# RMSNorm mean squares by a float32r product with a matrix of ones, and the last norm's scalings placed between the last products, in a two-layer hybrid decoder step

## The chip, the cores and the metric

The kernel runs on one core of a Trainium2 chip. The metric is the time of one execution on the device, in microseconds (us). A difference of 0.2% is about what can be told from none.

## What is computed

One inference step of a decoder with two layers, for a new sequence of 1024 tokens and eight samples of eight tokens, 1088 tokens in all, at a model width of 1024 in float32. Each layer is a token mixer (layer 0 an RG-LRU block with a convolution of width four, layer 1 chunked gated linear attention, GLA), a cross-attention over 256 memory tokens, and an MLP with a squared ReLU. In front of each of these six parts stands an RMSNorm, and one more at the end:

```python
def rmsnorm(x, g):
    y = x * lax.rsqrt(jnp.mean(x * x, axis=-1, keepdims=True) + EPS)
    return y * g

for layer in range(2):
    x = x + mixer[layer](rmsnorm(x, norm_mix_g[layer]))
    x = x + cross_attn(rmsnorm(x, norm_xa_g[layer]), mem_k[layer], mem_v[layer])
    x = x + square(relu(rmsnorm(x, norm_mlp_g[layer]) @ w1[layer])) @ w2[layer]
y = rmsnorm(x, final_norm_g)
```

A seventh norm of the same kind, of the memory, is made once at the start and isn't touched by the change.

## The kernel before

The residual `x` lies transposed in SBUF: 128 partitions by eight row tiles m (8 x 128 = 1024 features) by tokens, in three column blocks c of 384, 384 and 320 tokens (`x[c]`; the last holds 256 tokens of the sequence and the 64 of the samples). Products are made in three passes of float32r (`mm3`, L99 to L101): the high part of the weights (`whi`) by the high part of the data (`xh` or `hh`), by its low part (`xl`, `hl`), and the low part of the weights (`wlo`) by the high. Weights stream in as units of 512 KB, are split by ScalarE (L186, high) and VectorE (L187, low), and four split units are held at a time. A mixer's or MLP's out-product (`gemm_out`) is queued and run later, while the next in-product goes on; it adds each row tile into `x[c]` (L279) from one of three PSUM banks `pb`, so a bank is free for the next tile only when that add is done.

The norm is folded into the products: `norm_tile` (L297 on) squares a tile (ScalarE, L302 and L305), adds it to an accumulator `acc[c]` over the eight tiles (L306: GpSimd, and VectorE for tiles 3 and 7), and writes the tile times the gain g as `xh` (L311) and `xl` (L312). The inverse root is multiplied in behind the next product. It is made in two steps that `norm_end` puts into a queue of deferred calls (`after`, `tick`):

- `rstd_sum` (L332 to L341), two ticks later: for each 128 tokens a product of `acc` with the column `ones` (1/1024) sums over the partitions (L336) and leaves the mean squares by token, one per partition. `inv_rms` takes the inverse root of these few columns with Ln and Exp (ScalarE, L324 and L325) and one Newton step (VectorE, L327 to L330) into `rtok`.
- `rstd_row` (L343 to L351), one tick later: transposes of `rtok`, spread over 128 columns, give the same number on all partitions (L347), which ScalarE copies to `rstd[c]` (L348).

The last norm, V_FIN, has no product behind it. There `norm_tile` multiplies the gain into `x` itself (ScalarE, L309), and `finish` (L353 to L359) multiplies by `rstd[c]` tile by tile (L357: GpSimd for tiles 0 and 4, VectorE for the others) and stores four tiles at a time (L359: two stores of 768 KB for a wide block, of 640 KB for the last) from SyncE's queue. `mlp(1, V_FIN)` queues these last out-products; they run at the end one block after the other.

The order of instructions on an engine isn't the order of the Python calls: a scheduler places them by its own estimate of when their inputs are ready, unless a dependency forces an order.

## Time and profile before

| | |
|---|---|
| time, three runs | median 3048.1 us, 3046.98 to 3052.01 |
| the profiled execution | 3050.53 us |
| its span, first to last instruction | 3048.8 us |
| mean granted clock of TensorE | 0.994 of full speed |
| TensorE busy / weight loads busy | 98% / 96% of the span |
| VectorE / ScalarE / GpSimd busy | 57% / 34% / 6% |
| HBM traffic | 63 GB/s over the span |

The profile is that of one execution; its rows give starts in us from the span's first instruction, and durations. TensorE's matrix part is PE, its weight loads PEld, VectorE DVE, ScalarE ACT, GpSimd POOL, SyncE SP. Matrix instructions overlap in the pipeline, so a product's cost is read from the distance of two starts, not from its own duration. The granted clock is told as a share of full speed: 1.00 is 2.4 GHz, 0.50 is 1.2 GHz. A bracket behind a row gives the idle time of the engine before it and what ended it. L numbers are lines of the kernel before; the tables of instructions in the next section that are marked as the new order's have the lines of the changed file.

### The profile page before, as it was taken

Reading aid. Unit: us, or ns where it says so; the run is one execution under the profiler, and the core shown is the slowest. Engines: PE = TensorE matmul, PEld = TensorE weight load, DVE = VectorE, ACT = ScalarE, POOL = GpSimd, SP = SyncE. Lnnn points to the kernel's source line nnn. Section 1 sums busy time; section 2 is a strip of 40 time slices with the busy share of each in tenths; the row PEclk is TensorE's granted clock in tenths of the full one; section 3 lists DMA queues with packets and bytes.
Section 4 is the critical chain, followed back from the end, with each engine's and each line's share of the span. In section 5 each row is a group of like instructions: output and inputs, shape, how many; then the busy total and the mean of one; then the engine's idle time right before and its main releaser. Section 6 shows DMA issues by size and latency. Waiting matters only on the chain.

```text
span 3048.8 us, 45853 instructions
## 1 busy us (share of the span) xinstructions
PE 2999.3 (98%) x18923; PEld 2920.6 (96%) x18923; DVE 1752.6 (57%) x3304; ACT 1038.8 (34%) x1907; POOL 193.6 (6%) x267
## 2 busy tenths in 40 slices
PE   8999999999999999999999999999999999999997
PEld 8999999999999999999999999899999999999997
DVE  7577786566444444444664564765574444444445
ACT  7555573234121111112543343642251211112114
POOL 4100020001000000000200000100020000000002
PEclk9999999999999999999999999999999999999998
DMA  8311113332111111111211212143221111111111
GB/s 276 121 44 44 42 61 98 98 100 63 42 42 56 42 42 42 44 54 35 57 54 32 70 32 70 44 124 95 87 77 42 49 49 42 42 42 50 48 42 59
DMA packets 155778, 194.82 MB, mean 64 GB/s; under 512 B 11280, under 2 KB 140560, under 8 KB 155568
## 3 DMA queue, kind: packets, MB, share of 16 engines
q1 hardware_dynamic: 152768, 182.82, 19.5%
q0 software_dynamic: 2800, 9.06, 0.8%
q8 instruction: 148, 2.42, 0.3%
q14 instruction: 62, 0.51, 0.1%
HBM read 178.34 MB, written 13.52 MB: 63 GB/s over the span
## 4 chain that ended last, share of the span: by engine, by line
PE 91%; DVE 4%; ACT 2%; DMA 1%; issue 1%; POOL 0%; DVEq 0%; SPq 0%; ACTq 0%; POOLq 0%
PE pa L101 13%; PE pa L99 13%; PE pa L100 13%; PE pb L99 9%; PE pb L101 9%; PE pb L100 9%; PE pm L99 5%; PE pm L100 5%; PE pm L101 5%; PE pa L262 1%; DMA kvt<-in_cache_v 1%; PE pa L263 1%; PE pa L264 1%; DVE xl L312 1%; PE pb L800 1%
## 5 line engine op out<-in xcount | busy, mean ns | idle before, releaser
L99 PE MATMUL pa<-xh,whi 128*128 128x384 f32 (+2 forms) x2528 | 827.1, 327 | 0.7 <-ACT xh L311 0.7
L100 PE MATMUL pa<-xl,whi 128*128 128x384 f32 (+2 forms) x2528 | 825.1, 326 | 2.7 <-DVE xl L312 2.7
L101 PE MATMUL pa<-xh,wlo 128*128 128x384 f32 (+2 forms) x2528 | 827.4, 327 | 0.0
L279 DVE TENSOR_TENSOR x<-x,pb 128x384 f32<-128x384 f32 (+1 forms) x792 | 412.4, 528 | 209.4 <-PE pb L101 208.5
L99 PE MATMUL pb<-hh,whi 128*128 128x384 f32 (+1 forms) x1584 | 525.2, 332 | 3.2 <-DVE x L279 2.2
L101 PE MATMUL pb<-hh,wlo 128*128 128x384 f32 (+1 forms) x1584 | 519.6, 328 | 0.0
L100 PE MATMUL pb<-hl,whi 128*128 128x384 f32 (+1 forms) x1584 | 519.3, 328 | 0.0
L186 ACT CAST whi<-raw 128x1024 fp32r<-128x1024 f32 (+1 forms) x250 | 256.8, 1040 | 680.8 <-PE pa L100 357.7
L100 PEld LDWEIGHTS pa<-xl,whi 128*128 128x128 f32 x2528 | 475.7, 188 | 4.6 <-DVE xl L312 3.9
L99 PEld LDWEIGHTS pa<-xh,whi 128*128 128x128 f32 x2528 | 475.8, 188 | 2.6 <-ACT xh L311 1.0
L101 PEld LDWEIGHTS pa<-xh,wlo 128*128 128x128 f32 x2528 | 475.6, 188 | 1.0 <-DVE wlo L187 0.7
L187 DVE TENSOR_TENSOR wlo<-raw,whi 128x1024 fp32r<-128x1024 f32 (+1 forms) x250 | 304.6, 1229 | 242.2 <-ACT whi L186 239.3
L679 DVE SCALAR_TENSOR_TENSOR r<-pa,rstd 128x384 f32<-128x384 f32 (+1 forms) x192 | 102.3, 534 | 399.4 <-PE pa L101 398.7
L99 PEld LDWEIGHTS pb<-hh,whi 128*128 128x128 f32 x1584 | 299.0, 189 | 13.2 <-DVE x L279 6.6
L680 ACT ACTIVATE r<-r 128x768 f32<-128x768 f32 (+1 forms) x96 | 77.6, 808 | 674.4 <-DVE r L679 674.4
L100 PEld LDWEIGHTS pb<-hl,whi 128*128 128x128 f32 x1584 | 298.9, 189 | 0.3 <-DVE hl L546 0.3
L101 PEld LDWEIGHTS pb<-hh,wlo 128*128 128x128 f32 x1584 | 298.7, 189 | 0.1
L279 DVE TENSOR_TENSOR x<-x,pm 128x320 f32<-128x320 f32 (+1 forms) x360 | 190.9, 530 | 111.7 <-PE pm L101 111.6
L306 POOL TENSOR_TENSOR acc<-acc,sq 128x384 f32<-128x384 f32 (+1 forms) x105 | 118.1, 1125 | 2055.0 <-ACT sq L305 2040.8
L99 PE MATMUL pm<-hh,whi 128*128 128x320 f32 (+1 forms) x720 | 234.8, 326 | 0.0
L101 PE MATMUL pm<-hh,wlo 128*128 128x320 f32 (+1 forms) x720 | 234.8, 326 | 0.0
L100 PE MATMUL pm<-hl,whi 128*128 128x320 f32 (+1 forms) x720 | 234.7, 326 | 0.0
(310 smaller groups left out, 3940.0 us busy)
## 6 DMA issues: line engine op xcount, KB each, us to landing
raw<-in_mlp_w SPq DMA_DIRECT2D x128, 512.0 KB, 3.8
kvt<-in_cache_kT SPq DMA_DIRECT2D x64, 256.0 KB, 4.9
kvt<-in_cache_v SPq DMA_DIRECT2D x64, 256.0 KB, 5.0
raw<-in_xa_wv SPq DMA_DIRECT2D x16, 512.0 KB, 5.0
raw<-in_rg_w_in SPq DMA_DIRECT2D x16, 512.0 KB, 3.6
raw<-in_xa_wq SPq DMA_DIRECT2D x16, 512.0 KB, 3.5
raw<-in_xa_wo SPq DMA_DIRECT2D x16, 512.0 KB, 3.6
raw<-in_gla_w_in SPq DMA_DIRECT2D x16, 512.0 KB, 3.7
```

The lines of the kernel that those rows point to most:

```text
L99: mm(out, lh, rh, start=first, stop=False)
L100: mm(out, lh, rl, start=False, stop=False)
L101: mm(out, ll, rh, start=False, stop=last)
L186: nc.scalar.copy(hi[:, o], raw[:, o])
L187: nc.vector.tensor_sub(lo[:, o], raw[:, o], f32(hi[:, o]))
L262: mm(out, self.xh[c][:, k, xs], hv[:, kk, :], start=k == 0, stop=False)
L263: mm(out, self.xh[c][:, k, xs], lv[:, kk, :], start=False, stop=False)
L264: mm(out, self.xl[c][:, k, xs], hv[:, kk, :], start=False, stop=k == 7)
L279: nc.vector.tensor_add(x, x, p[:, :per * w].rearrange("p (m t) -> p m t", m=per))
L306: (nc.vector if m % 4 == 3 else nc.gpsimd).tensor_add(self.acc[c][:, :w], self.acc[c][:, :w], sq[:, :w])
L679: nc.vector.scalar_tensor_tensor(r[:, f], p[f][:, :w], 0.0, self.rstd[c], op0=OP.max, op1=OP.mult)
L680: nc.scalar.activation(r, r, AF.Square)
```

## The change

For the six inner norms the sum over the partitions is made by a square matrix of ones (`ones_r`, 128 x 128, value 1/1024) in float32r: `acc` is split into a high part `ah` (ScalarE) and a low part `al` (VectorE), two products of the block's width put the mean squares by token on all 128 partitions at once, and Ln, Exp and a Newton step in three operations of the block's width make `rstd[c]` directly. There is no `rtok` and there are no transposes; GLA's norm (V_MIX + 1), whose values are scaled by token, takes `rtok` back from `rstd` with one column of the identity (`rstd_col`). A forced order without a semaphore (`in_order`) keeps the first of the two products behind the last `mm3` issued before it.

The last norm is rearranged. Blocks 0 and 1 keep the old sum and transposes (`tok_sum`, `tok_row`), but these and the scalings (`piece`) are called from a table between the row tiles of the next block's out-product: block 0's between those of block 1 and the first of block 2, block 1's sum and transposes between those of block 2. The last block takes a full-precision product with the square of ones, and its scalings follow, behind block 1's. The gain is multiplied in together with `rstd` by one VectorE operation (L418 of the new file); only the tiles scaled by GpSimd (`on_pool`: 0 and 4 of block 0; 0, 2, 4 and 6 of block 1) still have it multiplied in by ScalarE. Block 1's accumulations are all GpSimd's. Stores are of two tiles: twelve of 393 or 328 KB (768 and 640 KB halved) where there were six.

```diff
         mm(out, lh, rl, start=False, stop=False)
-        mm(out, ll, rh, start=False, stop=last)
+        self.last_mm = mm(out, ll, rh, start=False, stop=last)
...
                     self.norm_tile(c, m, norm)
+                    if norm == V_FIN and c:
+                        self.between[c, m]()
         if last:
...
             nc.scalar.activation(sq[:, :w], x, AF.Square)
-            (nc.vector if m % 4 == 3 else nc.gpsimd).tensor_add(self.acc[c][:, :w], self.acc[c][:, :w], sq[:, :w])
+            self.last_acc = (nc.vector if m % 4 == 3 and (c, norm) != (1, V_FIN) else nc.gpsimd).tensor_add(self.acc[c][:, :w], self.acc[c][:, :w], sq[:, :w])
         g = self.vec[:, m, norm:norm + 1]
         if norm == V_FIN:
-            nc.scalar.activation(x, x, AF.Copy, scale=g)
+            if self.on_pool(c, m):
+                nc.scalar.activation(x, x, AF.Copy, scale=g)
         else:
...
         self.normed[c] = norm
-        self.after(2, lambda: self.rstd_sum(c, norm))
+        if norm != V_FIN:
+            self.after(2, lambda: self.rstd_sum(c, norm))
+        elif c == 0:
+            self.after(2, lambda: self.tok_sum(0))
+            self.last_pieces()
+        elif c == NC - 1:
+            self.rstd_sum(c, norm)
...
+        nc, w = self.nc, WID[c]
+        acc, r = self.acc[c][:, :w], self.rstd[c]
+        p = self.pm()[:, :w]
+        if norm == V_FIN:
+            nc.tensor.matmul(p, f32(self.ones_r), acc, start=True, stop=True)
+            for m in range(NK):
+                self.piece(1, m)
+        else:
+            ah, al = (self.sp.tile([128, MAXW], R32, name=n, tag="sq", bufs=2)[:, :w] for n in ("ah", "al"))
+            nc.scalar.copy(ah, acc)
+            nc.vector.tensor_sub(al, acc, f32(ah))
+            self.in_order(nc.tensor.matmul(p, self.ones_r, ah, start=True, stop=False))
+            nc.tensor.matmul(p, self.ones_r, al, start=False, stop=True)
+        nc.scalar.activation(r, p, AF.Ln, bias=self.eps)
+        nc.scalar.activation(r, r, AF.Exp, scale=-0.5)
+        u = self.sp.tile([128, MAXW], F32, name="nu", tag="acc", bufs=2)[:, :w]
+        nc.vector.scalar_tensor_tensor(u, p, EPS, r, op0=OP.add, op1=OP.mult)
+        nc.vector.scalar_tensor_tensor(u, u, -0.5, r, op0=OP.mult, op1=OP.mult)
+        nc.vector.scalar_tensor_tensor(r, u, 1.5, r, op0=OP.add, op1=OP.mult)
+        if norm == V_MIX + 1:
+            self.after(1, lambda: self.rstd_col(c, norm))
+            return
+        self.rstd_done[c] = norm
+        if norm == V_FIN:
+            self.finish(c)
+    def rstd_col(self, c, norm):
...
         for i, (j, t0, tw) in enumerate(TILES[c]):
-            nc.tensor.matmul(p[:tw, i:i + 1], self.acc[c][:, t0:t0 + tw], self.ones, start=True, stop=True)
+            nc.tensor.matmul(p[:tw, i:i + 1], self.rstd[c][:, t0:t0 + tw], self.ident[:, 0:1], start=True, stop=True)
+        j0, n = TILES[c][0][0], len(PTILES[c])
+        nc.vector.tensor_copy(self.rtok[:, j0:j0 + n], p[:, 0:n])
+        if c == NC - 1:
+            nc.vector.tensor_copy(self.rtok[:64, 8:9], p[:64, n:n + 1])
+        self.rstd_done[c] = norm
+    def in_order(self, mm):
+        if self.last_mm is not None:
+            self.tc.add_manual_dep(mm.ins, self.last_mm.ins.name, mybir.DependencyInfo(
+                mybir.DependencyClass.NoSync, mybir.DependencyReason.DATA), reason="order")
+    def tok_sum(self, c):
+        nc = self.nc
+        p = self.pm()
+        for i, (j, t0, tw) in enumerate(TILES[c]):
+            mm = nc.tensor.matmul(p[:tw, i:i + 1], self.acc[c][:, t0:t0 + tw], self.ones, start=True, stop=True)
+            if i == 0:
+                self.in_order(mm)
         j0, n = TILES[c][0][0], len(PTILES[c])
         self.inv_rms(self.rtok[:, j0:j0 + n], p[:, 0:n], 128, n)
-        if c == NC - 1:
-            self.inv_rms(self.rtok[:, 8:9], p[:64, n:n + 1], 64, 1)
-        self.after(1, lambda: self.rstd_row(c, norm))
-    def rstd_row(self, c, norm):
+    def tok_row(self, c):
         nc, w = self.nc, WID[c]
         p = self.pm()
-        for j, t0, tw in TILES[c]:
-            nc.tensor.transpose(p[:, t0:t0 + tw], self.rtok[:tw, j:j + 1].to_broadcast([tw, 128]), self.ident[:tw, :tw])
+        for i, (j, t0, tw) in enumerate(TILES[c]):
+            mm = nc.tensor.transpose(p[:, t0:t0 + tw], self.rtok[:tw, j:j + 1].to_broadcast([tw, 128]), self.ident[:tw, :tw])
+            if i == 0:
+                self.in_order(mm)
         nc.scalar.copy(self.rstd[c], p[:, :w])
-        self.rstd_done[c] = norm
-        if norm == V_FIN:
-            self.finish(c)
+    def on_pool(self, c, m):
+        return c < 2 and m % (4, 2)[c] == 0
+    def piece(self, c, m):
+        nc, w = self.nc, WID[c]
+        x = self.x[c][:, m, :]
+        if self.on_pool(c, m):
+            nc.gpsimd.tensor_mul(x, x, self.rstd[c])
+        else:
+            mul = nc.vector.scalar_tensor_tensor(x, x, self.vec[:, m, V_FIN:V_FIN + 1], self.rstd[c], op0=OP.mult, op1=OP.mult)
+            if c == 1:
+                self.tc.add_manual_dep(mul.ins, self.last_acc.ins.name, mybir.DependencyInfo(
+                    mybir.DependencyClass.NoSync, mybir.DependencyReason.DATA), reason="order")
+        if m % 2:
+            nc.sync.dma_start(self.a.yT[:, m - 1:m + 1, COL[c]:COL[c] + w], self.x[c][:, m - 1:m + 1, :])
+    def last_pieces(self):
+        do = lambda m: lambda: self.piece(0, m)
+        no = lambda: None
+        first = [no, lambda: self.tok_row(0), no, do(0), do(1), do(2), do(4), do(3)]
+        then = [do(5), no, do(6), no, lambda: self.tok_sum(1), do(7), lambda: self.tok_row(1), no]
+        self.between = {(c, m): fn for c, fns in ((1, first), (2, then)) for m, fn in enumerate(fns)}
     def finish(self, c):
-        nc, w = self.nc, WID[c]
         for m in range(NK):
-            x = self.x[c][:, m, :]
-            (nc.vector if m % 4 else nc.gpsimd).tensor_mul(x, x, self.rstd[c])
-            if m % 4 == 3:
-                nc.sync.dma_start(self.a.yT[:, m - 3:m + 1, COL[c]:COL[c] + w], self.x[c][:, m - 3:m + 1, :])
+            self.piece(c, m)
...
         make_identity(nc, self.ident)
-        self.ones = cp.tile([128, 1], F32, name="ones")
-        nc.vector.memset(self.ones, 1.0 / D)
+        self.ones_r = cp.tile([128, 128], R32, name="ones_r")
+        nc.vector.memset(f32(self.ones_r), 1.0 / D)
+        self.ones = f32(self.ones_r)[:, 0:1]
+        self.last_mm = None
         self.eps = cp.tile([128, 1], F32, name="eps")
```

How the change moves instructions is shown at three places, as the built programs have them, one row for each instruction or for equal ones in a row, first before and then now.

TensorE at the first norm end, that of block 0 of the first norm, among the products of the memory's keys (`mh`, `ml` are the memory's halves, `whi`, `wlo` the weights', `acc` the summed squares). Before:

```order
L459 MATMUL pa<-wlo,mh 128x256
L460 MATMUL pa<-whi,ml 128x256
L336 MATMUL pm<-ones,acc 128x1 x3
L458 MATMUL pb<-whi,mh 128x256
L459 MATMUL pb<-wlo,mh 128x256
```

and now, with the lines of the new file (L537 to L539 are the old L458 to L460):

```order
L538 MATMUL pa<-wlo,mh 128x256
L539 MATMUL pa<-whi,ml 128x256
L354 MATMUL pm<-ah,ones_r 128x384
L355 MATMUL pm<-al,ones_r 128x384
L537 MATMUL pb<-whi,mh 128x256
L538 MATMUL pb<-wlo,mh 128x256
```

The three products of one column are now two of 384 columns, at the same place; the transposes some fifty products later have no row any more.

ScalarE where the first gates of the RG-LRU layer are computed (L600, new L679: sigmoids into `rt`, `it`) and the last block's root of the first norm (`irms`, `rtok`; now `rstd`) falls between. Before:

```order
L324 ACTIVATE irms<-pm,eps 128x2
L325 ACTIVATE rtok<-irms 128x2
L600 ACT_TABLE_LOAD
L600 ACTIVATE rt<-pm,vec 128x384
L324 ACT_TABLE_LOAD
L324 ACTIVATE irms<-pm,eps 64x1
L600 ACT_TABLE_LOAD
L600 ACTIVATE it<-pm,vec 128x384
L325 ACT_TABLE_LOAD
L325 ACTIVATE rtok<-irms 64x1
L586 CAST xch<-xc 128x768
L600 ACT_TABLE_LOAD
```

and now:

```order
L665 CAST xch<-xc 128x768
L356 ACTIVATE rstd_97<-pm,eps 128x320
L357 ACTIVATE rstd_97<-rstd_97 128x320
L679 ACT_TABLE_LOAD
L679 ACTIVATE rt<-pm,vec 128x384
L679 ACTIVATE it<-pm,vec 128x384
L679 ACTIVATE rt<-pm,vec 128x384
L679 ACTIVATE it<-pm,vec 128x384
L684 ACT_TABLE_LOAD
```

Logarithm and exponential of the root now stand ahead of the first load, and the four sigmoids behind it in a row; over the whole program there are 50 loads where there were 54.

VectorE in the last products (`x_86`, `x_87`, `x_88` are blocks 0, 1 and 2 of the residual, `pb` the products' banks). Before, block 0's scalings (L357) stood together behind block 1's adds (L279):

```order
L279 TENSOR_TENSOR x_87<-x_87,pb 128x384 x3
L357 TENSOR_TENSOR x_86<-x_86,rstd_95 128x384 x3
L306 TENSOR_TENSOR acc<-acc,sq 128x384
L357 TENSOR_TENSOR x_86<-x_86,rstd_95 128x384 x3
L279 TENSOR_TENSOR x_88<-x_88,pb 128x320 x3
L327 SCALAR_TENSOR_TENSOR irms_28554<-pm,rtok 128x3
L279 TENSOR_TENSOR x_88<-x_88,pb 128x320
L328 TENSOR_TENSOR irms_28554<-irms_28554,rtok 128x3
```

and now they go between the adds (L418), behind the split of `r` into `hl`; the last two rows, one scaling and one add, come six times over in all:

```order
L339 TENSOR_TENSOR rtok<-rtok,irms_28227 128x3
L279 TENSOR_TENSOR x_87<-x_87,pb 128x384
L761 TENSOR_TENSOR hl<-r,hh 128x2x320
L279 TENSOR_TENSOR x_87<-x_87,pb 128x384
L418 SCALAR_TENSOR_TENSOR x_86<-x_86,vec,rstd_95 128x384
L279 TENSOR_TENSOR x_87<-x_87,pb 128x384
```

At the very end VectorE now runs:

```order
L339 TENSOR_TENSOR rtok<-rtok,irms_28399 128x3
L279 TENSOR_TENSOR x_88<-x_88,pb 128x320 x2
L308 TENSOR_TENSOR acc<-acc,sq 128x320
L418 SCALAR_TENSOR_TENSOR x_87<-x_87,vec,rstd_96 128x384 x4
L360 SCALAR_TENSOR_TENSOR nu<-pm,rstd_97 128x320
L361 SCALAR_TENSOR_TENSOR nu<-nu,rstd_97 128x320
L362 SCALAR_TENSOR_TENSOR rstd_97<-nu,rstd_97 128x320
L418 SCALAR_TENSOR_TENSOR x_88<-x_88,vec,rstd_97 128x320 x8
```

The scalings of block 0 are through before block 2's adds begin, and all eight of block 2 are VectorE's.

## Rows read from the trace of the kernel before

**Rows 1.** The page, engines: busy us, share, instructions.

```profile
PE 2999.3 (98%) x18923; PEld 2920.6 (96%) x18923; DVE 1752.6 (57%) x3304; ACT 1038.8 (34%) x1907; POOL 193.6 (6%) x267
```

**Rows 2.** Timeline, TensorE near 450 us: start, us, operation, out<-in, shape, count.

```profile
449.97 0.33 PE L101 MATMUL pa<-xh,wlo 128*128 128x384 f32 x1
450.14 0.72 PE L336 MATMUL pm<-ones,acc 128*128 128x1 f32 x6
450.73 0.40 PE L99 MATMUL pb<-hh,whi 128*128 128x320 f32 x1
```

**Rows 3.** Timeline, TensorE near 453 and 739 us.

```profile
453.04 0.51 PE L347 MATMUL pm<-ident,rtok 128*128 128x128 f32 x3
453.39 0.71 PE L774 MATMUL pm<-ident,P 128*128 128x128 f32 x5
...
739.07 0.58 PE L347 MATMUL pm<-ident,rtok 128*128 128x128 f32 x3
739.58 0.41 PE L99 MATMUL pa<-xh,whi 128*128 128x320 f32 x1
```

**Rows 4.** Timeline, TensorE near 52 us; brackets: idle time, releaser.

```profile
52.23 0.87 PE L347 MATMUL pm<-ident,rtok 128*128 128x128 f32 x3 [3.79 <-DVE rtok L330]
52.75 0.56 PE L458 MATMUL pa<-whi,mh 128*128 128x256 f32 x1
```

**Rows 5.** Windows: us, busy (count) PE, PEld, DVE, ACT, POOL, PEclk, DMA, GB/s.

```profile
48.00:52.00 4.00, 0.44 (x4) 0.24 (x3) 4.00 (x8) 4.00 (x10) 2.89 (x3) 0.98 1.02 334
52.00:55.20 3.20, 2.97 (x14) 3.00 (x15) 3.20 (x7) 2.72 (x6) 1.36 (x2) 0.50 0.71 232
...
154.00:161.00 7.00, 6.11 (x19) 5.79 (x20) 7.00 (x21) 5.62 (x9) 1.31 (x4) 0.52 0.48 150
```

**Rows 6.** Timeline, TensorE near 153 us.

```profile
153.09 0.45 PE L99 MATMUL pm<-xch,gwh 128*128 128x384 f32 x1 [3.00 <-ACT rt L600]
...
154.89 0.69 PE L99 MATMUL pb<-hh,whi 128*128 128x384 f32 x1 [1.00 <-ACT hh L545]
```

**Rows 7.** Timeline, TensorE at the last sum.

```profile
3031.45 1.14 PE L336 MATMUL pm<-ones,acc 128*128 128x1 f32 x6 [1.79 <-DVE acc L306]
```

**Rows 8.** Weight load of L336 near 713 us; L336's idle time (us, times).

```profile
713.04 0.30 PEld L336 LDWEIGHTS pm<-ones,acc 128*128 128x128 f32 x2 [0.50 <-DVE acc L306]
...
  DVE acc L306: 10.6, 8
```

**Rows 9.** Timeline, ScalarE, 130 to 138 us: first and last table load.

```profile
132.30 1.28 ACT L324 ACT_TABLE_LOAD   x1
...
138.01 1.28 ACT L600 ACT_TABLE_LOAD   x1
```

**Rows 10.** Groups by shape, ScalarE and VectorE: busy us, mean ns.

```profile
L186 ACT CAST whi<-raw 128x1024 fp32r<-128x1024 f32 x246 | 254.3, 1047 | 680.3 <-PE pa L100 357.7 <-PE pb L100 120.3 <-PE pm L100 116.0
...
L279 DVE TENSOR_TENSOR x<-x,pb 128x320 f32<-128x320 f32 x264 | 125.7, 484 | 83.3 <-PE pb L101 83.2
...
L306 DVE TENSOR_TENSOR acc<-acc,sq 128x384 f32<-128x384 f32 x28 | 15.3, 548 | 2.6 <-POOL acc L306 2.4
```

**Rows 11.** Timelines, TensorE and VectorE near 42 us.

```profile
41.92 0.72 PE L336 MATMUL pm<-ones,acc 128*128 128x1 f32 x6
...
41.78 1.13 DVE L312 SCALAR_TENSOR_TENSOR xl<-x,vec,xh 128x384 fp32r<-128x384 f32 x2
```

**Rows 12.** Timelines, VectorE and GpSimd, the last 33 us.

```profile
3016.24 3.76 DVE L357 TENSOR_TENSOR x<-x,rstd 128x384 f32<-128x384 f32 x3 [0.68 <-ACT rstd L348]
...
3039.85 3.83 DVE L357 TENSOR_TENSOR x<-x,rstd 128x320 f32<-128x320 f32 x6 [0.91 <-ACT rstd L348]
...
3017.00 2.59 POOL L357 TENSOR_TENSOR x<-x,rstd 128x384 f32<-128x384 f32 x2
```

**Rows 13.** DMA, 3010 to 3060 us: GB/s in 40 slices; KB, us to landing.

```profile
GB/s 0 7 0 0 0 0 0 0 64 374 355 372 93 0 0 0 0 0 0 0 7 0 182 355 379 343 80 347 362 260 0 0 0 0 0 0 0 0 0 0
...
out_yT<-x SPq DMA_DIRECT2D x2, 640.0 KB, 3.6
```


## The prediction

> **What bounds the kernel now.** I read the page first: TensorE is busy for 98% of the span [rows 1], so what TensorE no longer does, or no longer waits for, comes off the time almost one for one. Then I went to the norms. Each of the seven norms ends once per column block (c = 0, 1, 2), 21 times. In the timeline of TensorE such an end has two pieces: three products with the one-column `ones`, which hold TensorE from 450.14 to 450.73 us, 0.59 us [rows 2], and some us later three transposes, 0.35 us where all rows are 128 wide and 0.51 us for the block with 64 rows [rows 3]. Ordinary products of 384 columns start 0.17 us apart [rows 2]. Next come the places where TensorE stands still. At 52 us it waits 3.79 us for `rtok` of the first block [rows 4], and the granted clock is then 0.50 up to 55.2 [rows 5]. At 153.1 and 154.9 it waits 3.00 and 1.00 us for ScalarE [rows 6], and until 161 the clock is 0.52 [rows 5]. Last is the end of the kernel: from the last sum at 3031.45 [rows 7] to 3048.8 there is only the last norm, 17.4 us.
>
> **The change, part by part.** The 18 ends of the six norms before the last:
>
> *Sums and transposes removed.* 18 x 0.59 = 10.6 us, and at two places (the second block of each MLP norm; the first stands there) the weight load waited 0.50 us for the accumulator [rows 8], of which I count 0.4 each: 11.4. The transposes: 12 x 0.35 + 6 x 0.51 = 7.3, and the wait of 3.79 at 52 us: 11.1. Together 22.5 us.
>
> *Products added.* Two float32r products per end, of the form and width of the ordinary ones: 18 x 2 x 0.17 = 6.1 us. Where the inverse root is also wanted by token (three ends, V_MIX + 1), three column products are left, 3 x 0.59 = 1.8. The net is 22.5 - 7.9 = **-14.6 us**.
>
> *The clock at 52 us.* If that wait is gone, the 2.4 us behind the transposes at 0.50 run at full clock: **-1.2**.
>
> *ScalarE's table loads at the first gates.* In the old order the last block's roots are threaded between sigmoids, and ScalarE reloads its tables: four loads of 1.28 us from 132.30 to 138.01 that the new order doesn't have [rows 9]; the order shows one load and then four gates. From there ScalarE works almost without a pause, up to the gates that TensorE waits for at 153. 4 x 1.28 = 5.1 us earlier is more than the waits of 4.0, so I let them go, and with them the low clock, 7.0 x 0.48 = 3.4: **-7.4**. Its bounds are 0 (another late operand takes their place) and -7.4.
>
> *New waits for the split accumulator.* The sum now needs `ah` (a cast on ScalarE; 1024 columns take 1.05 us, so I put 384 at 0.5) and `al` (VectorE, 0.55) behind the finished accumulator [rows 10], 1.1 us more, and it is held behind the products issued before it, so TensorE stands if they are late. At the first end TensorE reaches the sum at 41.92, while VectorE has two `xl` up to 42.9 in front of `al` [rows 11]: 42.9 + 0.55 gives 1.6 us. VectorE is then busy without a gap until 52 [rows 5], and the change gives it three operations of 384 columns (1.65 us by the same row) for four tiny ones, so part of the 3.79 returns as a wait for split weights, between 0 and 3.79; I take 1.5, since TensorE had its weights at 52.75 [rows 4]. At four places (the first block of layer 0's attention norm and the MLP ends of rows 8) the accumulator is done hardly before the sum; the new order puts products between, so 0.5 each, 2.0. Sum **+5.1**, bounds +1 and +9. Elsewhere the accumulator is ready and VectorE and ScalarE, 57% and 34% busy [rows 1], take the wider root beside TensorE; without that cover each end would cost its 1.1 us.
>
> *The end.* Six of block 0's eight scalings now go to VectorE between block 1's adds, while GpSimd runs two scalings and seven accumulations in a row. What that costs is in the trace: three such VectorE operations beside GpSimd took 3.76 us, 1.25 each, against 0.55 for one alone [rows 12, 10]. Six at 1.25, sixteen adds near 0.5 (0.48 the narrow ones [rows 10]), the split of `r` and the small roots make some 19 us of VectorE from 3007 on, so the last sum comes near 3030 where it was 3031.45: -1.5. Behind the sum: block 1's four VectorE scalings beside GpSimd's four (5.0) cover the product, Ln and Exp; then three root operations (1.5), eight scalings at 0.49 (3.9) and the last store. Now the last scaling ends at 3043.7 [rows 12] and the span 5.1 us later; a store of 320 instead of 640 KB at the 360 GB/s of the strip [rows 13] takes 0.9 less, 4.2. 5.0 + 1.5 + 3.9 + 4.2 = 14.6 against 17.4: -2.8. Together **-4.3**. The bounds are 0 and, if nothing contends, -11.9: six scalings at 0.55 bring the sum 4.2 earlier, and behind it 0.6 for the product and 1.0 for Ln and Exp stand in place of the 5.0. TensorE's own waits inside the last products are in this, since VectorE sets the pace of both.
>
> *Smaller stores.* Twelve issues for six. The rows are still 1280 and 1536 bytes long, and two stores in a row moved without a hole at 340 to 380 GB/s [rows 13], so I cost the extra six at nothing; if that cover were gone, rival C is the price. [...]
>
> *Sum.* -14.6 - 1.2 - 7.4 + 5.1 - 4.3 = -22.4. The profiled run took 3050.5, which gives 3028.1; it lay 2.4 above the median of the runs, of which I take off one: **3027 us**.
>
> **The rivals.**
> A. The gates' stall only moves: TensorE arrives there some 5 us earlier too, and VectorE or a weight split is late instead. Without the 7.4: 3034. For it: VectorE had no gap from 154 to 161 [rows 5]. Against: the waits name ScalarE [rows 6].
> B. The end gives nothing, because VectorE and GpSimd lock step through all of blocks 1 and 2 and the clock falls in the gaps, as it does now: 3027 + 4.3 = 3031, up to 3 more.
> C. Each small store pays its fixed part in turn. A store of 640 KB lands after 3.6 us [rows 13], 1.8 of it moving; four stores of 1.8 + 0.9 in turn are 10.8, about 6 more than I have: 3033. [...]
> D. **Slower.** TensorE stands at each of the 18 sums, because `ah` waits behind a weight split of 1.05 [rows 10] on ScalarE: 1.05 + 1.1 = 2.2 us, 18 times 40 us, against gains of 27.5 in all. That gives 3050 + 12 = 3062. It decides from a mean wait of 1.5 us on. For it: the forced place, and rows 8. Against: the accumulator was waited for in eight entries only, matrix and weight loads counted apart [rows 8], those at 3020 and 3031 among them.
> E. The change hardly does what it says: the first stage is held by VectorE, the gates don't gain, the end doesn't either: -14.6 + 9 = 3045, no difference that can be told.
>
> **How the numbers follow.** Forecast 0.61, A 0.15, B 0.10, C 0.03, E 0.06, D 0.05. Below 3042 (0.2%, about what a measurement of this kernel tells from none) lie the forecast, A, B and C: faster 0.89; same 0.06 (E); slower 0.05 (D). The lower bounds together (-14.6 - 1.2 - 7.4 + 1 - 11.9, and the one us) give 3015; upward the range takes in A with B, 3039, and leaves out D and E. So 3014 to 3039.
>
> **What would show it.** Right: the sum's two products 0.34 us on TensorE and no transposes between 50 and 2300 us; no wait above 2 us at 52; four table loads fewer, and no wait for the gates near 150; the last store landing some 14 to 15 us behind the last sum. Wrong: waits of more than 1 us before the `al` product at many of the 18 ends (D), a fall of the clock near 45 or 150 us, or scalings of 1.2 us that push the adds of block 2 past 3028 on VectorE.

## The result, and the profile after

The changed kernel takes 3029.3 us (median of four runs, 3028.2 to 3034.0), the kernel before 3048.8 (four runs, 3047.0 to 3052.0): a ratio of 0.9938 with a 95% interval of 0.9926 to 0.9950, or 19.5 us less. The forecast was 3027, its range 3014 to 3039. The profiled execution of the changed kernel is the longest of the four, 3034.0 us with a span of 3032.3; where that matters below, a second trace stands beside it.

The page's engines, where before had [rows 1]:

```profile
PE 2984.3 (98%) x18808; PEld 2902.5 (96%) x18808; DVE 1775.2 (59%) x3277; ACT 1033.9 (34%) x1870; POOL 193.0 (6%) x269
```

TensorE still bounds the kernel. The first norm end, where [rows 2] had three column products and [rows 4] the wait, and the same stretches as [rows 5], with one more:

```profile
41.74 0.34 PE L354 MATMUL pm<-ah,ones_r 128*128 128x384 f32 x1
42.75 0.44 PE L355 MATMUL pm<-al,ones_r 128*128 128x384 f32 x1 [0.67 <-DVE al L353]
...
438.33 0.34 PE L354 MATMUL pm<-ah,ones_r 128*128 128x384 f32 x1
438.50 0.34 PE L355 MATMUL pm<-al,ones_r 128*128 128x384 f32 x1
438.68 0.49 PE L853 MATMUL pm<-ident,P 128*128 128x128 f32 x3
```

```profile
48.00:52.00 4.00, 4.00 (x36) 4.00 (x35) 3.56 (x6) 3.59 (x8) 3.06 (x3) 1.00 1.02 329
52.00:55.20 3.20, 3.20 (x29) 3.20 (x29) 3.20 (x3) 1.76 (x3) 3.08 (x2) 1.00 0.87 286
154.00:161.00 7.00, 7.00 (x48) 7.00 (x47) 5.59 (x8) 6.86 (x8) 0.98 (x1) 1.00 0.00 0
1455.50:1459.00 3.50, 3.50 (x15) 3.50 (x15) 3.09 (x7) 2.87 (x6) 1.71 (x2) 0.51 0.77 258
```

The three early stretches are full, at full clock; the fourth is discussed below. The two products start 0.17 us apart like their neighbours. But there are waits where before had none:

```profile
129.60 0.44 PE L99 MATMUL pm<-xch,gwh 128*128 128x384 f32 x1 [2.22 <-DVE nu L360]
...
700.85 0.44 PE L354 MATMUL pm<-ah,ones_r 128*128 128x384 f32 x1 [0.54 <-ACT ah L352]
702.16 0.45 PE L355 MATMUL pm<-al,ones_r 128*128 128x384 f32 x1 [0.28 <-DVE al L353]
718.82 0.41 PE L354 MATMUL pm<-ah,ones_r 128*128 128x320 f32 x1 [0.94 <-ACT ah L352]
...
1454.62 0.83 PE L375 MATMUL pm<-ident,rstd 128*128 128x1 f32 x6 [2.25 <-DVE rstd L362]
```

At the gates a product wants a bank that still holds the mean squares, until VectorE reads them (L360). The MLP norm ends wait for `ah` and `al` (layer 1 has the same three waits). In front of the GLA the column products wait for the wide root, and the clock falls to 0.51 behind that.

The end (VectorE, TensorE, GpSimd), for [rows 7] and [rows 12], and the DMA strip from 3010 to 3060 for [rows 13]:

```profile
3007.58 0.90 DVE L418 SCALAR_TENSOR_TENSOR x<-x,vec,rstd 128x384 f32<-128x384 f32 x1
...
3019.02 4.41 DVE L418 SCALAR_TENSOR_TENSOR x<-x,vec,rstd 128x384 f32<-128x384 f32 x4
3023.35 0.48 DVE L360 SCALAR_TENSOR_TENSOR nu<-pm,rstd 128x320 f32<-128x320 f32 x1
...
3024.92 3.79 DVE L418 SCALAR_TENSOR_TENSOR x<-x,vec,rstd 128x320 f32<-128x320 f32 x8
...
3019.15 1.44 PE L347 MATMUL pm<-acc,ones_r 128*128 128x320 f32 x2 [2.13 <-DVE acc L308]
...
3017.75 4.73 POOL L416 TENSOR_TENSOR x<-x,rstd 128x384 f32<-128x384 f32 x4
```

```profile
GB/s 147 0 0 0 0 7 0 0 0 315 315 322 307 182 342 354 170 0 0 0 0 0 0 0 0 0 0 0 0 0 0 0 0 0 0 0 0 0 0 0
```

The last sum starts at 3019.15 and the span ends 13.15 us later, where it was 17.35. Where the time came from is read from leads: the start of a product in the trace of before less the start of the same product in another trace. The products are third products of `mm3` (L101), of which every trace has 5264; six of them and the span's end are in the table:

| us, before | 124.3 | 208.7 | 797.6 | 1611.8 | 2348.8 | 3029.35, last | span's end |
|---|---|---|---|---|---|---|---|
| changed kernel | 4.8 | 10.8 | 12.1 | 9.0 | 9.4 | 12.6 | 16.5 |
| e1_inner | 5.5 | 10.1 | 12.9 | 12.2 | 13.2 | 13.8 | 14.2 |
| e2_tail | -1.0 | 0.1 | 0.4 | 0.4 | 1.3 | 4.6 | 8.4 |
| e3_gates | -2.4 | 4.2 | 3.9 | 3.9 | 4.6 | 6.0 | 6.3 |
| e4d_gla_old | 5.1 | 12.3 | 15.0 | 15.9 | 17.5 | 20.8 | 24.6 |
| e10_best | 6.1 | 13.5 | 16.3 | 17.2 | 17.2 | 21.1 | 26.5 |

A lead comes from one trace of each kernel, and unchanged code differs too: e2_tail and e3_gates have the first norm's sums as before up to 124.3 and are 1.0 and 2.4 us behind there; from 2348.8 to the end, e1_inner and e3_gates run the old last norm and gain 1.0 and 1.7.

### The profile page after: what moved, and what is told of

It is laid out like the page before. It is cut to its first block, busy times and chain, and to the rows that moved or that the text cites. A ratio compares the mean times of both kernels' runs of the same rounds, so it can differ in the third digit from the quotient of the medians.

```text
span 3032.3 us, 45545 instructions
## 1 busy us (share of the span) xinstructions
PE 2984.3 (98%) x18808; PEld 2902.5 (96%) x18808; DVE 1775.2 (59%) x3277; ACT 1033.9 (34%) x1870; POOL 193.0 (6%) x269
## 4 chain that ended last, share of the span: by engine, by line
PE 85%; DVE 6%; DMA 3%; ACT 3%; issue 2%; POOL 1%; SPq 0%; DVEq 0%; ACTq 0%; POOLq 0%
PE pa L101 12%; PE pa L100 12%; PE pa L99 12%; PE pb L99 8%; PE pb L101 8%; PE pb L100 8%; PE pm L99 5%; PE pm L100 5%; PE pm L101 4%; DVE xl L315 1%; PE pa L262 1%; PE pa L263 1%; PE pa L264 1%; DVE wlo L187 1%; ACT whi L186 1%
## 5 line engine op out<-in xcount | busy, mean ns | idle before, releaser
L101 PE MATMUL pa<-xh,wlo 128*128 128x384 f32 (+2 forms) x2528 | 825.8, 327 | 0.0
L279 DVE TENSOR_TENSOR x<-x,pb 128x384 f32<-128x384 f32 (+1 forms) x792 | 412.1, 528 | 205.5 <-PE pb L101 204.8
L101 PE MATMUL pb<-hh,wlo 128*128 128x384 f32 (+1 forms) x1584 | 518.2, 327 | 0.0
L101 PEld LDWEIGHTS pa<-xh,wlo 128*128 128x128 f32 x2528 | 474.6, 188 | 0.9 <-DVE wlo L187 0.6
L101 PEld LDWEIGHTS pb<-hh,wlo 128*128 128x128 f32 x1584 | 297.7, 188 | 0.0
L279 DVE TENSOR_TENSOR x<-x,pm 128x320 f32<-128x320 f32 (+1 forms) x360 | 190.6, 529 | 109.2 <-PE pm L101 109.2
L101 PE MATMUL pm<-hh,wlo 128*128 128x320 f32 (+1 forms) x720 | 234.5, 326 | 0.0
```

The source lines that it names most:

```text
L101: self.last_mm = mm(out, ll, rh, start=False, stop=last)
L279: nc.vector.tensor_add(x, x, p[:, :per * w].rearrange("p (m t) -> p m t", m=per))
```

## The experiments

Theory: the gain is the sum of the prediction's terms, TensorE's products and stalls in the inner norms and VectorE's work at the end, and what is short of it was lost to VectorE, which the wide root loads. Rivals: the stalls only move (A); the end gives nothing (B); small stores cost (C); the forced place makes TensorE stand (D). The edits are shown in excerpt.

**The halves.** `e1_inner` has the changed inner norms and the last norm of before (sums, transposes, `finish` and stores of four tiles, here called `fin_sum`), `e2_tail` the reverse. The first edit is against the kernel before, the second against the changed one, where `rstd_sum` and `rstd_row` are also put back as they were:

```diff
-        self.after(2, lambda: self.rstd_sum(c, norm))
+        if norm != V_FIN:
+            self.after(2, lambda: self.rstd_sum(c, norm))
+        else:
+            self.after(2, lambda: self.fin_sum(c, norm))
```

```diff
         elif c == NC - 1:
-            self.rstd_sum(c, norm)
+            self.last_sum(c, norm)
```

> The six inner norms as in the changed kernel, the last norm as before. In the two profiles the changed kernel leads by 9.4 us when the first sum of the last norm starts, and by 16.5 us at the end. If the two parts add up as they stand there, this kernel takes 3048.8 - 9.4 = 3039 us or a few less, with the lead of 9 to 10 us at the first sum of the last norm. Rival: the end gives nothing by itself and only shows what the inner norms gained; then this kernel is as fast as the changed one, 3029 to 3031.

> The inner norms as before, the last norm as in the changed kernel: sums, scalings and stores of two tiles between the last products. If the end is worth what the two profiles show behind the first sum of the last norm, 16.5 - 9.4 = 7.1 us, this takes 3048.8 - 7.1 = 3042 us; my term of 4.3 us would give 3044.5; a rival in which the end gives nothing gives 3049. Together with the other half the sum should come to the 19.5 us of the whole change within 3 us; if not, the halves depend on each other.

Measured: e1_inner 3035.0 us, ratio 0.9952 (0.9940 to 0.9965), 14 us; e2_tail 3042.8, ratio 0.9977 (0.9968 to 0.9985), 6 to 7 us. The halves add up to the whole within 2 us, and the end gives something by itself: B falls. Both numbers of the first expectation were off (3039, and 3029 to 3031), since they went by the changed kernel's own, long, execution. By the table the end is worth 7.1 us (from 2348.8 on) in the changed kernel and in e2_tail alike, with the 1 to 2 us of uncertainty named above.

**The table loads.** In the kernel before:

```diff
-        nc.scalar.activation(r, t[:rows, cs], AF.Exp, scale=-0.5)
+        self.last_exp = nc.scalar.activation(r, t[:rows, cs], AF.Exp, scale=-0.5)
...
-                    nc.scalar.activation(d[:, f], p[:, :w], AF.Sigmoid, ...)
+                    s = nc.scalar.activation(d[:, f], p[:, :w], AF.Sigmoid, ...)
+                    if (g, c) == (0, 0):
+                        self.tc.add_manual_dep(s.ins, self.last_exp.ins.name, ...)
```

> The kernel before with one thing changed: the first four sigmoids of the RG-LRU layer are ordered behind the last Exp of the first norm, so that ScalarE loads its tables four times fewer, 50 for 54. Theory of the forecast: the waits of 3.00 and 1.00 us near 153 us and the half clock behind them come from these loads, and go: 3048.8 - 7.4 = 3041.4. Rival: VectorE or a weight split is late in their place and the stall only moves: 3047 to 3049. The last block's mean squares are still made the old way here, with the transposes.

Measured: 3042.8 us, ratio 0.9982 (0.9973 to 0.9991), a gain of 5.5 to 6. ScalarE, then the windows view of the stretch that [rows 5] have at 0.52:

```profile
135.15 0.20 ACT L325 ACTIVATE rtok<-irms 64x1 f32<-64x1 f32 x1
135.37 1.28 ACT L600 ACT_TABLE_LOAD   x1
136.66 0.58 ACT L600 ACTIVATE rt<-pm,vec 128x384 f32<-128x384 f32 x1
```

```profile
154.00:161.00 7.00, 7.00 (x40) 6.88 (x40) 7.00 (x23) 6.88 (x13) 1.21 (x4) 1.00 0.39 126
```

The stall and the low clock are gone with the four loads, although VectorE is busy without a gap in that stretch, which rival A had given as its reason. From 124.3 to 208.7 the lead grows by 6.6 us; the term had 7.4. A falls: the stall didn't move.

**GLA's root.** `e4d_gla_old` makes that one norm the old way (`gla_sum` is the old `rstd_sum`); `e4b_order` only moves its column products:

```diff
-            self.after(2, lambda: self.rstd_sum(c, norm))
+            self.after(2, lambda: (self.gla_sum if norm == V_MIX + 1 else self.rstd_sum)(c, norm))
```

```diff
+                self.last_mm = mm(out, self.xl[c][:, k, xs], hv[:, kk, :], start=False, stop=k == 7)
...
+            if i == 0:
+                self.in_order(mm)
```

> The changed kernel, with the norm in front of the GLA (layer 1) alone made the old way: column sums, small roots, transposes. On TensorE that is even, since this norm needs column products in either form. Theory: the 2.4 us that TensorE stands at 1454.6 us, and the half clock behind them, come from the three wide root operations that stand in VectorE's queue behind a weight split and beside GpSimd's constants; then the loss of 3.2 us there (lead of 12.1 us before, 8.9 behind) goes, and the time is 3029.3 - 3 = 3026. Rival: VectorE is late there anyway, for the residual's adds, and TensorE waits for a bank instead: 3028.5 to 3029.5, the lead behind that place still near 9.

> The changed kernel, with GLA's three column products (those that take the root by token out of the wide root) forced behind the last token product issued before them; the built order puts block 0's eighteen out-products later than now. It asks whose fault the wait at 1454.6 us is. If only the place of the column products is wrong (TensorE could go on with the out-products), the wait goes: as good as e4d_gla_old, which keeps its lead over that place (-15.0 us before it, -16.2 behind), 3026 to 3028. If VectorE is what is late there, with the wide root and the residual's adds in one queue, the out-products wait for a bank in place of the column products: the lead falls by 1 to 3 us over that place as in the changed kernel, 3029.

Measured: e4d_gla_old 3027.8 us, ratio 0.9929 (0.9917 to 0.9942); e4b_order 3030.7, ratio 0.9938 (0.9924 to 0.9952). The time alone doesn't separate the first from the changed kernel (0.9938); the traces do. Between 797.6 and 1611.8 the changed kernel loses 3.1 us of lead, e4d_gla_old gains 0.9. In e4b_order TensorE waits at the same place for as long, for a bank:

```profile
1456.14 0.44 PE L99 MATMUL pb<-hh,whi 128*128 128x384 f32 x1 [2.16 <-DVE x L279]
```

So VectorE is what is late, and the place of the column products isn't at fault. VectorE of the changed kernel there:

```profile
1450.39 1.23 DVE L187 TENSOR_TENSOR wlo<-raw,whi 128x1024 fp32r<-128x1024 f32 x1 [0.86 <-ACT whi L186]
1451.54 0.65 DVE L361 SCALAR_TENSOR_TENSOR nu<-nu,rstd 128x384 f32<-128x384 f32 x1
1452.11 0.60 DVE L315 SCALAR_TENSOR_TENSOR xl<-x,vec,xh 128x384 fp32r<-128x384 f32 x1
1452.64 1.93 DVE L362 SCALAR_TENSOR_TENSOR rstd<-nu,rstd 128x384 f32<-128x384 f32 x1
1454.49 0.60 DVE L315 SCALAR_TENSOR_TENSOR xl<-x,vec,xh 128x384 fp32r<-128x384 f32 x1
1455.02 1.47 DVE L279 TENSOR_TENSOR x<-x,pb 128x384 f32<-128x384 f32 x3
```

The root's second operation stands behind a weight split that waits for ScalarE, the third takes 1.93 us where one takes 0.5 to 0.6, and the adds that free TensorE's banks come behind both. The loss differs from trace to trace: 1.9 us between 1390 and 1467 us in e1_inner, e7_stores4 and e8_no_pool, which have the same code there, 4.3 in the changed kernel's own trace, with the low clock. Part of that is luck of the order: in those three traces the same operation takes 0.55, and the long one is the `xl` behind it, for which no column product waits. So in e1_inner:

```profile
1451.69 0.55 DVE L351 SCALAR_TENSOR_TENSOR rstd<-nu,rstd 128x384 f32<-128x384 f32 x1
1452.16 1.95 DVE L312 SCALAR_TENSOR_TENSOR xl<-x,vec,xh 128x384 fp32r<-128x384 f32 x1
```

There TensorE waits 0.72 us for the column products and 0.45 for a bank, and the clock stays at full speed.

**The bank at the gates.** e4d_gla_old, and:

```diff
+        ms = p
+        if norm != V_FIN:
+            nc.scalar.copy(u, p)
+            ms = u
```

> The run e4d_gla_old with one more change: behind the Ln, ScalarE copies the mean squares of each inner norm from the PSUM bank to SBUF, and VectorE's first root operation reads the copy. Theory: the 2.2 to 2.4 us that TensorE stands near 129 us in the changed kernel (1.5 in e4d_gla_old) come from the bank that the wide root holds until VectorE, busy with the convolution, comes to it; then that wait goes and the time is 1.5 to 2.4 us under e4d_gla_old's 3027.8, some 3026. Rival: the bank isn't what is waited for, or the 15 copies of 0.5 us on ScalarE delay the casts that TensorE waits for; then no gain or up to 1 us of loss: 3028 to 3029.

Measured: 3026.8 us, ratio 0.9928 (0.9916 to 0.9941). In e4d_gla_old TensorE still waits there:

```profile
128.10 0.44 PE L99 MATMUL pm<-xch,gwh 128*128 128x384 f32 x1 [1.35 <-DVE nu L360]
```

With the copy it has no wait near 129 us, so the bank is the cause; the time isn't told apart from e4d_gla_old's.

**One tick less.**

```diff
-            self.after(2, lambda: self.rstd_sum(c, norm))
+            self.after(1, lambda: self.rstd_sum(c, norm))
```

> The changed kernel, the six inner norms' sums asked for one step of the deferred queue after the norm's end in place of two. It puts the prediction's rival D on trial: how much hangs on the distance between the accumulator's end and the place of the two products. If the forced place is what keeps TensorE from standing, the sums now come before ah and al are there, 1 to 2 us of waiting at most of the 18 ends, in all +15 to +35 us: 3045 to 3065. If the accumulator and its split are early enough anyway, no difference: 3028 to 3031.

Measured: 3042.0 us, ratio 0.9981 (0.9972 to 0.9990), 13 us more than the changed kernel. The idle time before L354 by releaser, in the changed kernel and here (matrix and weight loads counted apart):

```profile
  ACT ah L352: 7.2, 8
```

```profile
  ACT ah L352: 30.9, 21
```

The mechanism of rival D is real, and the two ticks are what keeps it away. Its price was too high: 13 us over 18 ends is 0.7 each, where D had 2.2.

**Stores of four tiles.**

```diff
-        if m % 2:
-            nc.sync.dma_start(self.a.yT[:, m - 1:m + 1, COL[c]:COL[c] + w], self.x[c][:, m - 1:m + 1, :])
+        if m % 4 == 3:
+            nc.sync.dma_start(self.a.yT[:, m - 3:m + 1, COL[c]:COL[c] + w], self.x[c][:, m - 3:m + 1, :])
```

> The changed kernel with stores of four tiles, six in place of twelve. By the prediction's term (no cost of the six extra issues, 0.9 us for the smaller last one) it is slower by 0.9 us, with 4.5 us from the last scaling to the end in the profile where the changed kernel has 3.6. By rival C (each small store pays its fixed part in turn) it is faster by up to 6 us, with the stretch behind the last scaling shorter or equal.

Measured: 3029.5 us, ratio 0.9940 (0.9924 to 0.9955). The last scalings, in a span of 3026.9:

```profile
3018.66 3.79 DVE L418 SCALAR_TENSOR_TENSOR x<-x,vec,rstd 128x320 f32<-128x320 f32 x8
```

From their end at 3022.45 to the span's end are 4.45 us, where the changed kernel has 3.6 (3028.7 to 3032.3): 0.85 for half a store, as the term had it. C falls: twice as many stores cost nothing at the end. The changed kernel's last four stores land 2.4 us after their issue (median, in the last column), but they overlap: four in turn would take 9.6 us, and from the end of block 2's second scaling (3024.92 + 2 x 0.47) to the span's end are 6.4.

```profile
out_yT<-x SPq DMA_DIRECT2D x4, 320.0 KB, 2.4
```

**No scalings on GpSimd.**

```diff
-        return c < 2 and m % (4, 2)[c] == 0
+        return False
```

> The changed kernel with all scalings of the last norm on VectorE: two more of block 0, four more of block 1, none on GpSimd, and no gain written by ScalarE. If the four scalings of block 1 cost 1.1 us each only because GpSimd works beside them (4.41 us in all), eight alone take 8 x 0.55 = 4.4, and the end comes at the same distance behind the last sum, 13 us; the two more in block 0 cost 1.1 us before it, so the time is the same or 1 us longer, 3029 to 3031. Rival: the duration is VectorE's own and GpSimd takes real work off it; then eight take 8.8 us and the end comes 4 us later or more: 3034 to 3036.

Measured: 3028.3 us, ratio 0.9933 (0.9920 to 0.9947), the same time.

```profile
3014.00 4.32 DVE L418 SCALAR_TENSOR_TENSOR x<-x,vec,rstd 128x384 f32<-128x384 f32 x8
```

Eight alone take 4.32 us, four beside GpSimd's four 4.41. The last sum starts at 3014.14 and the span ends 13.1 us later, as with GpSimd's help, which is worth nothing that shows here.

**One full-precision product for `ah` and `al`.**

```diff
-            self.in_order(nc.tensor.matmul(p, self.ones_r, ah, start=True, stop=False))
-            nc.tensor.matmul(p, self.ones_r, al, start=False, stop=True)
+            self.in_order(nc.tensor.matmul(p, f32(self.ones_r), acc, start=True, stop=True))
```

> The changed kernel with one full-precision product of the accumulator at each of the 18 inner ends, in place of the two float32r products of ah and al; ScalarE's cast and VectorE's subtraction go with them. The full-precision product of 320 columns takes some 0.6 us by its two records behind the last sum of the run e8_no_pool, 0.81 with the pipeline's end, so 384 columns some 0.7 where two float32r products take 0.34: 18 x 0.35 = 6 us more. What it gives back are waits: 0.83 us at the first end and 2.2 us in each MLP norm are in the changed kernel's trace, of which some 3 us hang on the split. So I expect +3, 3032. If the split's 1.1 us cost more than that (my term of 5.1 us for the new waits), it comes out even, 3029 to 3030; if the waits hang on the accumulator alone, +6, 3035.

Measured: 3029.1 us, ratio 0.9936 (0.9923 to 0.9949): even, not +3. TensorE at the second end:

```profile
66.36 0.28 PE L101 MATMUL pa<-xh,wlo 128*128 128x256 f32 x1
66.48 0.81 PE L351 MATMUL pm<-acc,ones_r 128*128 128x384 f32 x2
66.83 0.57 PE L99 MATMUL pb<-xh,whi 128*128 128x256 f32 x1
67.24 0.28 PE L100 MATMUL pb<-xl,whi 128*128 128x256 f32 x1
```

From 66.48 to 67.24, less 0.12 for the product between, it holds TensorE 0.64 us, 0.29 more than the two it replaces: at most 18 x 0.29 = 5.2 us, since six ends are narrower. The times alone don't say what came back for that, since each is known to some 4 us; the traces do. The first end has no wait any more, and in each MLP norm 0.7 us are left, most of it here, where the changed kernel lost 0.84 and 2.7:

```profile
700.61 0.91 PE L351 MATMUL pm<-acc,ones_r 128*128 128x384 f32 x2 [0.19 <-DVE acc L308]
```

So 0.84 + 2 x 2.0 = 4.8 us of waits hung on the split, close to what the longer products cost.

**Two versions from this.** `e10_best` joins e4d_gla_old, the copy of e5_early_bank for the first norm alone, and e8_no_pool, and sums the last square by a product of its own; `e11_best_mixed` adds the product of e9_unsplit at seven ends:

```diff
-            nc.tensor.matmul(p, f32(self.ones_r), acc, start=True, stop=True)
+            nc.tensor.matmul(p, f32(self.ones_r), acc, start=True, stop=False)
+            nc.tensor.matmul(p, f32(self.ones_r), self.last_sq, start=False, stop=True)
```

```diff
+            if norm in (V_MLP, V_MLP + 1) or (c, norm) == (0, V_MIX):
+                self.in_order(nc.tensor.matmul(p, f32(self.ones_r), acc, start=True, stop=True))
```

> A version of what the runs suggest: GLA's norm the old way (as in e4d_gla_old), the mean squares copied out of the bank by ScalarE for the first norm alone, all scalings on VectorE (as in e8_no_pool), and block 2's last square summed by a second product behind that of the accumulator, in place of an addition by VectorE. Against e4d_gla_old, 3027.8: 1.5 us for the wait near 129 us, 0.9 us for the addition of 0.9 that stands ahead of the last sum and of the scalings behind it: 3025.5. If the copies or the moved scalings take it back, 3027 to 3028.

> The run e10_best with one more change: at seven of its fifteen inner ends, the first one and the three of each MLP norm, the sum is one full-precision product of the accumulator, the others keep ah and al. In e9_unsplit such a product of 384 columns held TensorE 0.64 us at the first end (from 41.83 to 42.59, less the 0.12 of the product between), 0.29 more than the two float32r products. Against that, the split's ends in the changed kernel lost 1.3 us at the first end and 3.7 in each MLP norm, all three ends together, and e9_unsplit 0.64 and some 2.6. If these are the waits that hang on the split, the gain is 0.7 + 2 x 1.1 = 2.9 us: 3024.6 - 2.9 = 3021.7. If what e9_unsplit gained there was only moved to a later bank, 3024 to 3025.

Measured: e10_best 3024.6 us (3024.0 to 3027.9), ratio 0.9923 (0.9909 to 0.9937); e11_best_mixed 3025.5 (3021.2 to 3028.7), ratio 0.9927 (0.9913 to 0.9941). Each of e10_best's five runs lies under each of the changed kernel's four, though the intervals overlap: by the medians it is the best version here, 4.7 us under the changed kernel; the runs don't tell it from e4d_gla_old, e5_early_bank or e11_best_mixed. Its end, from 2348.8 on, is worth some 9 us by the table, 2 more than the changed kernel's: its scalings follow the last add at once:

```profile
3008.58 0.49 DVE L279 TENSOR_TENSOR x<-x,pb 128x320 f32<-128x320 f32 x1 [0.82 <-PE pb L101]
3008.99 4.45 DVE L432 SCALAR_TENSOR_TENSOR x<-x,vec,rstd 128x384 f32<-128x384 f32 x8
```

The mixed sums of e11_best_mixed bring nothing that shows in the time; its trace gains 1.1 us between 1611.8 and 2348.8, where e10_best has none, and is 2.3 us behind at 797.6, most of that from the first 125 us.

## Why the prediction was right, point by point

The mechanisms named for the products, the table loads and the stores held. That the time came within 2.3 us of the forecast is in part luck, since two terms were off in opposite directions.

- **Net products, -14.6, and the clock at 52 us, -1.2.** The transposes and the wait are gone, and the two products cost 0.17 us each: shown by the rows. The term can't be measured without the waits at the same ends: e1_inner's 14 us less the 5.5 to 6 of e3_gates leave some 8 for both, where the terms have 14.6 + 1.2 - 5.1 = 10.7. By the terms' shares the lead at 124.3 should have been 3.1 us (two ends, the wait of [rows 4] and the clock: 2 x 0.94 + 3.79 + 1.2, less 0.7 for the products and 1.6 and 1.5 of new waits); it was 4.3 to 6.1 in the eight traces with the new inner norms, split and asked for after two ticks, but two traces with the old ones are 1.0 and 2.4 us behind before there, so this is no sign of a larger gain.
- **Table loads, -7.4.** Right in mechanism, a little too large: e3_gates shows 6.6 in the trace, 5.5 to 6 in the time. In the changed kernel it is reduced by the wait of 2.22 at 129.6, which the prediction didn't have.
- **New waits, +5.1.** Near in size (6.2), wrong in place. The 1.5 us expected from 48 to 52 didn't come, the first end waits 0.84 (from 41.74 to 42.75, less 0.17) instead of 1.6, and the first block of layer 0's attention norm doesn't wait. The MLP norms lost more than "0.5 each": from the start of the product before each of the six products to that of the product behind, 4.65 us in all at the three ends of one norm, less 1.0 for these six and 1.0 for the products before them, 2.7, which makes 5.4 for both layers.
- **"Elsewhere ... VectorE and ScalarE, 57% and 34% busy, take the wider root beside TensorE."** This step failed. A mean over the span was used for two places where VectorE sets the pace: at 129 us, where the root's late reading holds a bank (2.2 us), and in front of the GLA, where the root and the adds share a queue (1.9 to 4.3 us). With the 1.1 us by which the new waits exceed their term that is 5.2 to 7.6 us, against the 4.1 by which the inner norms' 14 us fall short of the 18.1 that the terms without the end have. No single run takes all of it away, but where GLA's root is made the old way the lead at 2348.8 is 17.5 (e4d_gla_old) and 17.2 (e10_best).
- **The end, -4.3.** Right in direction, too small: 6 to 7 us, and partly for another reason. The sum came 2.9 us earlier than the rest of the kernel (lead of 9.4 at 2348.8, of 12.3 at the sum), against 1.5. The prediction took VectorE to set the pace and counted "some 19 us of VectorE from 3007 on"; these end at 3026, so "near 3030" and the 1.5 don't follow from them. From block 0's small root to the last sum, in the windows of before, then of the changed kernel:

```profile
3007.10:3031.45 24.35, 18.99 (x103) 18.34 (x101) 17.48 (x35) 17.34 (x37) 11.98 (x12) 0.86 0.18 65
```

```profile
2997.73:3019.15 21.42, 17.72 (x106) 15.74 (x104) 17.27 (x34) 12.62 (x26) 16.11 (x16) 0.99 0.20 74
```

  VectorE's busy time is the same, and it stands idle for more than 4 us of the new stretch. What differs is TensorE's clock, 0.86 and 0.99; at full clock the two stretches would be, as an estimate, 24.35 x 0.86 = 20.9 and 21.42 x 0.99 = 21.2 us. In before, TensorE waits for block 1's accumulator, whose last addition stands behind three scalings on VectorE ([rows 12], 3016.24 to 3020.00), and its clock is low behind that:

```profile
3020.53 0.83 PE L336 MATMUL pm<-ones,acc 128*128 128x1 f32 x6 [2.59 <-DVE acc L306]
```

```profile
3021.00:3028.00 7.00, 6.03 (x25) 5.94 (x25) 5.03 (x13) 4.50 (x11) 2.60 (x3) 0.53 0.62 225
```

  The prediction has this clock only in rival B and gives its return no price at the end; that the 2.9 us are the clock's is read from these rows, and no run changes it alone. The six scalings took 6.0 us (1.47 and five of 0.90) for 7.5. Behind the sum it is 13.15 us against 14.6: four scalings 4.41 for 5.0, the last store 3.6 for 4.2.
- **Smaller stores, 0.** Right, with the 0.9 for the smaller last one. Four fixed costs one after another, as in rival C, are not what the strip shows: queued stores run at 307 to 354 GB/s in it, with one slice of 182 where the last block's begin.

So the time was met with two errors that nearly cancel: 4 us too much for the inner norms, 2 to 3 too little for the end. Of the rivals, A, B and C fell by e3_gates, e2_tail and e7_stores4, E by the time itself; D is the one that the kernel's two ticks keep off.

## What to carry to other kernels

The share of an engine over the span doesn't say whether it can take more work beside another: look at it in each place where the work will fall, at what stands ahead of it in its queue, and at which buffers it holds until it gets there. A product in place of a small chain frees TensorE, but here it was even whether the input was split for two fast products or taken in full precision: the split's waits (4.8 us) cost about what its shorter products saved (at most 5.2). Where operations that switch ScalarE's tables are threaded among others by a scheduler, look for an ordering dependency first: here one was worth about as much (e3_gates, 5.5 to 6 us) as the whole rearranged end (e2_tail, 6 to 7).

## What was not expected

GpSimd's share in the last norm's scalings was worth nothing: eight scalings took 4.32 us on VectorE alone and 4.41 (VectorE) and 4.73 (GpSimd) when split four and four. The Trainium skill, "SBUF — State Buffer", "Who interferes with whom", says that only the port pair shared by these two engines contends, under an exclusive lock. The trace agrees that they contend, 1.10 us for a scaling beside GpSimd and 0.54 alone; how long each holds the other up isn't shown. It depends on the operation: beside GpSimd's accumulations a scaling, with both its tensors in SBUF, took 0.90 us, while the add next to it, with one of them in PSUM, kept its 0.54:

```profile
3007.11 0.54 DVE L279 TENSOR_TENSOR x<-x,pb 128x384 f32<-128x384 f32 x1
...
3002.87 10.46 POOL L308 TENSOR_TENSOR acc<-acc,sq 128x384 f32<-128x384 f32 x9
```

The root's 1.93 us in front of the GLA, where GpSimd builds constants and accumulates, may be the same; no run took GpSimd away there.

The full-precision product of 384 columns held TensorE 0.64 us, of which 0.29 fell on the product behind it: the distance to the next start alone (0.35) would have shown it as cheap as two float32r products.
